# A decoder block in fp32: the row sums of four modulation vectors, as fp32 products in the array's column groups

## The chip, the cores and the metric

The kernel runs on one core of a Trainium2 chip (trn2). A core has five engines that run side by side and wait for one another by semaphores: TensorE (PE; its weight load is listed as PEld), VectorE (DVE), ScalarE (ACT), GpSimd (POOL) and SyncE (SP), which here only issues DMAs. The metric is device time in microseconds, from start to end of one execution.

## What is computed

A decoder block on 512 tokens of width 1024. A conditioning vector c gives six modulation vectors, each of 1024 elements, with a full matrix product per vector. Two of them (shift and scale of the first norm) are needed at once; the other four (g1, sh2, sc2, g2) only from the output projection on.

```python
c_act = jax.nn.silu(c)
mod = (c_act @ w_mod[l] + b_mod[l])[:, None, :]
sh1, sc1, g1, sh2, sc2, g2 = jnp.split(mod, N_MOD, axis=-1)
h = rms_norm(x) * (1.0 + sc1) + sh1
proj = h @ w_in[l]
u, v, z, xbc, dt_raw, gate_a, gate_b = jnp.split(proj, offs, axis=-1)
...
mixed = (jax.nn.sigmoid(gate_a) * (y_a @ w_branch_gm[l])
         + jax.nn.sigmoid(gate_b) * (y_b @ w_branch_ssm[l]))
x = x + g1 * (mixed @ w_out[l])
h2 = rms_norm(x) * (1.0 + sc2) + sh2
x = x + g2 * (jnp.square(jax.nn.relu(h2 @ w_ff1[l])) @ w_ff2[l])
```

## The kernel before

All large products run in three parts: a weight is split into a high part (wH, a cast by ScalarE) and a low part (wL, the difference, by VectorE, or by GpSimd for the weights in POOL_L), the activations likewise, and `mm3` adds high x high, high x low and low x high in PSUM. Weights come in pieces of 1 MB, two pieces ahead of their use (AHEAD = 2, line 26); `weight` (line 164) and `emit_w` (line 142) issue load, cast and difference. The pieces lie in a ring of three raw buffers (`rawt`), and the split halves in rings of four.

`projA` (line 180) makes one block of 128 output columns: 8 blocks of K, three products each, so 24 products of 512 columns. A piece of 256 columns gives two such blocks, called b = 0 and b = 1.

The stretch of the change is a loop over eight pieces: ("ga", 0), ("ga", 1), ("gm", 0), ("ga", 2), ("gm", 1), ("ga", 3), ("gm", 2), ("gm", 3). The "ga" pieces are the gate of the gMLP branch, the "gm" pieces its branch product. The SSM part follows, with pieces bc0, xs0, z0 and so on. Into this loop the remaining modulation vectors are woven: after block b = 0 of each piece `mod2(q)` (line 623) is called, with q = 0 to 7; each q is one half (512 elements) of one vector.

Small works are placed by hand: `later(n, fn)` (line 121) puts fn on a list, due n units from now; `tick` (line 124) advances the time by half a unit, in the middle and at the end of each projA, and runs what is due. So one unit is one projA, and one piece is two units. TensorE's instructions keep exactly the order in which the program issues them (class InOrder). VectorE, ScalarE and SP had that order forced for the first stage only; from then on a scheduler orders each engine's queue at compile time, by the order of issue and by what it takes to be ready. On the chip every queue is strictly in order.

`mod2(q)` before: two loads of 1 MB (w_mod rows 0 to 511 and 512 to 1023, 512 columns), in two of the three raw buffers; eight VectorE steps, each raw row block times a column of the activated c, added alternately to two accumulators; GpSimd adds the two (line 638). The partition sum is still to be taken. `finish`, three units later, splits the accumulator in m2H (ScalarE) and m2L (VectorE). `rows`, three units after that, multiplies both with a matrix of ones (two products of 512 columns), and VectorE adds the bias row br, and 1 for the sc2 vector. The row goes to DRAM, to `grow`, from where it is read back, spread over the partitions, before the output projection (line `g1row = rowload(grow[0], "g1")` and the next ones). br is loaded from b_mod in `mod2`.

Others that matter here. `dt_phase` (line 693) computes softplus and the running sum of dt by about twenty small VectorE steps, each dependent on the one before; it is issued right after `mod2(0)`. Its `to_tok` transposes the results (copies cumt and dtt), its `lasts` uses cumt. `mod_rows` (line 312) makes the first two modulation vectors at the start of the kernel by fp32 products in column groups: 32 columns of weights each, at `tile_position=(0, 32 * j)`. `decays` (line 779) has GpSimd subtract and mask the tile cum. PSUM has five banks for `mm` and three for `sx` (row sums, transposes, SSM).

Of the kernel before, what the change touches and what calls it, by code (L numbers as in the profile page):

```python
# [11 lines left out]
ALU = mybir.AluOpType  # L12
# [3 lines left out]
P = 128  # L16
S = 512
D = 1024
# [14 lines left out]
def hybrid_block(ctx: ExitStack, tc: tile.TileContext, x, c, w_mod, b_mod, w_in, gm_norm_w, gm_ws,  # L33
# [3 lines left out]
    pool = nc.gpsimd  # L37
# [20 lines left out]
    pe, dve, act = InOrder(nc.tensor, True), InOrder(nc.vector, True), InOrder(nc.scalar, True)  # L58
    sp = InOrder(nc.sync, True)
# [8 lines left out]
    def nm(s):  # L68
        uid[0] += 1
        return f"{s}_{uid[0]}"  # L70

    def const(shape, name, dt=F32):
        return cst.tile(shape, dt, tag=name, name=name)

    def blk(name, dt=F32, n=512):
        return big.tile([P, n], dt, tag="b", name=nm(name), bufs=NB)
# [7 lines left out]
    def rawt(name):  # L84
        return big.tile([P, 2048], F32, tag="raw", name=nm(name), bufs=3)
# [6 lines left out]
    def mm_bank():  # L92
        return psp.tile([P, 512], F32, tag="mm", name=nm("mm"), bufs=5)

    def sx_bank():
        return psp.tile([P, 512], F32, tag="sx", name=nm("sx"), bufs=3)
# [7 lines left out]
    def stt(o, a, s, b, op0, op1):  # L104
        dve.scalar_tensor_tensor(o, in0=a, scalar=s, in1=b, op0=op0, op1=op1)

    def low(L, src, H, eng=None):
        (eng or dve).tensor_tensor(L, in0=src, in1=H.bitcast(F32), op=ALU.subtract)  # L108

    def split(src, name):  # L110
        H, L = blk(name + "H", F32R), blk(name + "L", F32R)
        act.copy(H, src)
        low(L, src, H)
        return H, L

    mm, tr = pe.matmul, pe.transpose
# [4 lines left out]
    def later(n, fn):  # L121
        pend.append((unit[0] + n, fn))
# [88 lines left out]
    for f in range(2):  # L211
        for j in range(8):
            c0 = f * 2048 + j * 256
# [39 lines left out]
    ones = const([P, P], "ones")  # L253
# [3 lines left out]
    onesr = const([P, P], "onesr", F32R)  # L257
# [39 lines left out]
    cact = const([P, KB], "cact")  # L297
# [49 lines left out]
    def mod_sum(k):  # L347
        ps = sx_bank()
        for a in range(2):
            mm(ps[:, a:a + 1], lhsT=accm[k][:, a * P:(a + 1) * P], rhs=ones[:, 0:1], start=True, stop=True)  # L350
        return ps
# [147 lines left out]
    for k in range(1, KB - 1):  # L499
# [18 lines left out]
        else:  # L518
            mains(k, 2, B7)
            ps = mod_sum(k + 1)  # L520
# [53 lines left out]
    for h in range(2):  # L574
        w = weight(("v1", h)) if h else wv[0]
        for k in range(4):
            wh, wl = w(k, 0, 512)
            kk = 4 * h + k
# [38 lines left out]

    grow = drm.tile([4, D], F32, name="grow")

    def small_row(name):  # L620
        return blk(name)[0:1, :]

    def mod2(q):
        which, half = divmod(q, 2)
        c0 = (2 + which) * D + half * 512
        acc = [blk("acc"), blk("acc")]
        for j2 in range(2):
            raw = rawt("mod2").rearrange("p (k n) -> p k n", k=4)
            sp.dma_start(raw, w_mod[0][j2 * 512:(j2 + 1) * 512, c0:c0 + 512].rearrange("(k p) n -> p k n", p=P))
            for j in range(4):  # L630
                kk = j2 * 4 + j
                a = acc[j % 2]
                if kk < 2:
                    dve.tensor_scalar(a, in0=raw[:, j], scalar1=cact[:, kk:kk + 1], scalar2=None, op0=ALU.mult)
                else:
                    stt(a, raw[:, j], cact[:, kk:kk + 1], a, ALU.mult, ALU.add)

        pool.tensor_tensor(acc[0], in0=acc[0], in1=acc[1], op=ALU.add)
        br = small_row("br")
        sp.dma_start(br, b_mod[0:1, c0:c0 + 512])  # L640

        def finish():
            H, L = split(acc[0], "m2")
            later(3, lambda: rows(H, L))

        def rows(H, L):
            ps = sx_bank()
            mm(ps, lhsT=onesr, rhs=H, start=True, stop=False)
            mm(ps, lhsT=onesr, rhs=L, start=False, stop=True)
            stt(br, ps[0:1, :], 1.0 if which == 2 else 0.0, br, ALU.add, ALU.add)  # L650
            sp.dma_start(grow[which:which + 1, half * 512:(half + 1) * 512], br)
        later(3, finish)


    yaH, yaL = [None] * 8, [None] * 8
# [19 lines left out]
    for j in range(3):  # L675
        w = weight(("u", j))
        for b in range(2):
            ps = mm_bank()
# [69 lines left out]
    for kind, j in (("ga", 0), ("ga", 1), ("gm", 0), ("ga", 2), ("gm", 1), ("ga", 3), ("gm", 2), ("gm", 3)):  # L748
        w = weight((kind, j))
        for b in range(2):  # L750
            m = 2 * j + b
            ps = mm_bank()
            if kind == "ga":
                projA(ps, w, b * P, hH, hL)
                ga[m] = blk("ga")
                act.activation(ga[m], ps, AF.Sigmoid)
            else:
                projA(ps, w, b * P, yaH, yaL)
                pa[m] = ga[m]
                mul(ga[m], ps, ga[m])  # L760
            if b == 0:
                mod2(nmod[0])
                nmod[0] += 1
            tick()
# [167 lines left out]
    for j in range(4):  # L932
        w = weight(("gb", j))
        for b in range(2):
            ps = mm_bank()
# [14 lines left out]
    for j in range(4):  # L950
# [5 lines left out]
        for b in range(2):  # L956
# [3 lines left out]
            H, L = split(gb[m], "mx")  # L960
# [62 lines left out]
    for t in range(NT):  # L1023
        ps = mm_bank()
# [44 lines left out]
    for f in range(2):  # L1069
# [13 lines left out]
        for j in range(j0, 8):  # L1083
            w = weight(("f1", f, j))
            for b in range(2):
                ps = mm_bank()
# [4 lines left out]
        for n in range(2):  # L1091
# [4 lines left out]
            for qp in range(2):  # L1096
# [7 lines left out]
                for k, (t, i, c0, c1) in steps:  # L1104
                    wh, wl = ws[k // 4](k % 4, c0, c1)
                    kk = 8 * qp + k
# [38 lines left out]
```

## Time and profile before

| what | value |
|---|---|
| median of 3 runs | 1098.85 us (1096.06 to 1101.81) |
| profiled execution | 1096.96 us |
| its span, first to last instruction | 1095.3 us |
| mean granted TensorE clock | 0.997 of full speed |
| busy: PE, DVE, ACT, POOL | 98%, 60%, 44%, 17% of the span |

The profile is one execution. "Busy" counts the time in which an engine has an instruction in it; products overlap in the array, so that 512 columns are listed with 390 ns and yet follow one another every 0.23 us. "PE sx L49" means an instruction of TensorE that writes a bank named sx; most lines are 49, the line of the helper that records all operations, so groups are told apart by their tiles. In the chain (the work that ended last, followed back) each piece is released by the one before it. "x48" means that 48 instructions are drawn together in one row; the time is then from the first one's start to the last one's end. In brackets stands the idle time before, and what ended it.

### The profile page before, as it was taken

How to read it: one execution, taken by the hardware profiler on the slowest of the kernel's cores; microseconds unless marked ns; L12 is line 12 of the kernel's file. 1: busy time of each engine (PE TensorE's matmuls, PEld its weight loads, DVE VectorE, ACT ScalarE, POOL GpSimd, SP SyncE). 2: the span in 40 equal slices, each digit the busy share in tenths (PEclk: the TensorE clock that was granted, in tenths of full speed). 3: DMA queues.
4: the chain of work that ended last, by engine and by line, in shares of the span. 5: the costliest groups of instructions: out<-in, count | busy, mean ns of one | idle time of the engine just before them, and what ended most of it. 6: DMA issues, size and time to landing. Idle time of an engine off the chain costs nothing.

```text
span 1095.3 us, 13316 instructions
## 1 busy us (share of the span) xinstructions
PE 1075.7 (98%) x5330; PEld 895.6 (82%) x5330; DVE 652.2 (60%) x897; ACT 482.5 (44%) x637; POOL 186.5 (17%) x131
## 2 busy tenths in 40 slices
PE   8999999999999999999999999989999999999997
PEld 7788887888888888888888888878888888888886
DVE  4854699976687677687757434385443425444244
ACT  5557345355665655655537222233432112433122
POOL 0030743132431431431110000350000000000000
PEclk9999999999999999999999999999999999999999
DMA  9863257985343333333333234313232323232302
GB/s 296 261 196 97 75 180 271 316 257 166 116 126 107 116 125 106 116 125 106 106 115 115 77 116 135 115 43 116 93 112 81 113 80 116 77 115 96 115 1 78
DMA packets 122623, 141.67 MB, mean 129 GB/s; under 512 B 3664, under 2 KB 93856, under 8 KB 122560
## 3 DMA queue, kind: packets, MB, share of 16 engines
q1 hardware_dynamic: 120768, 137.09, 39.9%
q10 hardware_dynamic: 1152, 2.10, 0.5%
q0 software_dynamic: 640, 1.63, 0.5%
q8 instruction: 42, 0.69, 0.3%
q14 instruction: 21, 0.17, 0.0%
HBM read 138.55 MB, written 2.24 MB: 129 GB/s over the span
## 4 chain that ended last, share of the span: by engine, by line
PE 90%; DVE 6%; DMA 2%; ACT 1%; issue 1%; POOL 0%; DVEq 0%; ACTq 0%; POOLq 0%
PE mm L49 75%; PE sx L49 15%; DMA mod<-in_w_mod_dram 1%; DVE xn L49 1%; DVE acc L49 1%; DVE e L49 1%; DMA brow<-in_b_mod_dram 0%; DVE xr L49 0%; POOL wL L108 0%; DVE q L49 0%; ACT junk L49 0%; DVE ss L49 0%; DVE h L49 0%; DVE s L49 0%; ACT h L49 0%
## 5 line engine op out<-in xcount | busy, mean ns | idle before, releaser
L49 PE MATMUL mm<-h,wH 128*128 128x512 f32 (+1 forms) x1712 | 521.6, 386 | 0.0
L49 PEld LDWEIGHTS mm<-h,wH 128*128 128x128 f32 x1712 | 312.8, 189 | 61.0 <-issue 2.7
L49 PE MATMUL mm<-h,wL 128*128 128x512 f32 (+1 forms) x856 | 327.9, 383 | 1.4 <-POOL wL L108 1.4
L49 DVE TENSOR_TENSOR wL<-raw,wH 128x1024 fp32r<-128x1024 f32 x154 | 194.0, 1263 | 207.0 <-ACT wH L49 206.8
L49 ACT CAST wH<-raw 128x1024 fp32r<-128x1024 f32 x170 | 177.5, 1049 | 294.2 <-PE mm L49 223.6
L49 PEld LDWEIGHTS mm<-h,wL 128*128 128x128 f32 x856 | 161.3, 188 | 34.0 <-POOL wL L108 1.6
L49 ACT ACT_TABLE_LOAD x64 | 82.1, 1283 | 6.2 <-issue 3.0
L49 DVE SCALAR_TENSOR_TENSOR cv<-mm,wcol,cv 128x511 f32<-128x511 f32 (+2 forms) x96 | 70.9, 743 | 13.7 <-ACT cv L49 13.1
L49 PE MATMUL mm<-wL,aH 128*128 128x512 f32 (+1 forms) x176 | 66.8, 380 | 0.0
L49 PE MATMUL mm<-wH,aH 128*128 128x512 f32 (+1 forms) x176 | 66.8, 380 | 0.0
L49 PE MATMUL mm<-wH,aL 128*128 128x512 f32 (+1 forms) x176 | 66.8, 379 | 0.0
L108 POOL TENSOR_TENSOR wL<-raw,wH 128x1024 fp32r<-128x1024 f32 x16 | 40.7, 2548 | 130.7 <-ACT wH L49 130.5
L794 POOL TENSOR_TENSOR cum<-cum,cumt 128x1024 f32<-128x1024 f32 x16 | 34.7, 2166 | 71.5 <-DMA cum<-cumd 58.3
L49 DVE TENSOR_TENSOR r<-r 128x512 f32<-128x512 f32 x32 | 22.0, 688 | 35.7 <-ACT r L49 35.7
L49 PE MATMUL mm<-wH,h 128*128 128x512 f32 x128 | 40.2, 401 | 0.9 <-ACT h L49 0.9
L49 PE MATMUL mm<-y,wH 128*128 128x512 f32 x128 | 39.4, 389 | 0.0
L49 PEld LDWEIGHTS mm<-wH,aL 128*128 128x128 f32 x176 | 33.1, 188 | 6.3
L49 PEld LDWEIGHTS mm<-wH,aH 128*128 128x128 f32 x176 | 33.1, 188 | 5.9
L49 PEld LDWEIGHTS mm<-wL,aH 128*128 128x128 f32 x176 | 33.1, 188 | 5.9
L49 ACT ACTIVATE r<-mm 128x512 f32<-128x512 f32 x32 | 19.0, 594 | 39.5 <-PE mm L49 39.5
L49 DVE SCALAR_TENSOR_TENSOR acc<-mod,cact,acc 128x512 f32<-128x512 f32 x48 | 35.5, 791 | 0.5 <-DMA mod<-in_w_mod_dram 0.5
L49 PE MATMUL sx<-wL,aH 128*128 128x512 f32 (+1 forms) x96 | 35.7, 372 | 0.0
(236 smaller groups left out, 1519.2 us busy)
## 6 DMA issues: line engine op xcount, KB each, us to landing
raw<-in_w_ff_dram SPq DMA_DIRECT2D x32, 1024.0 KB, 5.1
raw<-in_w_in_dram SPq DMA_DIRECT2D x28, 1024.0 KB, 5.5
mod<-in_w_mod_dram SPq DMA_DIRECT2D x16, 1024.0 KB, 7.0
raw<-in_w_in_dram SPq DMA_DIRECT2D x18, 512.0 KB, 4.1
mod<-in_w_mod_dram SPq DMA_DIRECT2D x16, 512.0 KB, 7.3
cum<-cumd SPq DMA_DIRECT2D x16, 512.0 KB
raw<-in_w_branch_ssm_dram SPq DMA_DIRECT2D x8, 1024.0 KB, 5.2
raw<-in_w_branch_gm_dram SPq DMA_DIRECT2D x4, 1024.0 KB, 6.1
```

The source lines that it names most:

```text
L49: r = fn(*a, **k)
L108: (eng or dve).tensor_tensor(L, in0=src, in1=H.bitcast(F32), op=ALU.subtract)
L794: pool.tensor_tensor(cv, in0=cv, in1=ct, op=ALU.subtract)
```

## The change

Each q now has one accumulator: the first step writes it, the other seven add to it, one after another. GpSimd's sum, the split in m2H and m2L and the function `finish` are gone. After q = 3 and after q = 7, three units later, `rows` takes four accumulators at once: four fp32 products, each with a 128 x 32 matrix of ones, in the four column groups, all into one bank; so vector j of the four stands in partitions 32j to 32j + 31. One VectorE step over 128 partitions adds the four bias rows and `plus1`, a small constant that holds 1 for the sc2 rows. The four bias rows are now loaded within `rows`, each spread over 32 partitions, and four rows go to `grow`.

```diff
-    def small_row(name):
-        return blk(name)[0:1, :]
+    plus1 = const([P, 2], "plus1")
+    pool.memset(plus1, 0.0)
+    pool.memset(plus1[0:64, 1:2], 1.0)
...
-        acc = [blk("acc"), blk("acc")]
+        acc = blk("acc")
...
-                a = acc[j % 2]
-                if kk < 2:
-                    dve.tensor_scalar(a, in0=raw[:, j], scalar1=cact[:, kk:kk + 1], scalar2=None, op0=ALU.mult)
+                if kk == 0:
+                    dve.tensor_scalar(acc, in0=raw[:, j], scalar1=cact[:, kk:kk + 1], scalar2=None, op0=ALU.mult)
                 else:
-                    stt(a, raw[:, j], cact[:, kk:kk + 1], a, ALU.mult, ALU.add)
-
-        pool.tensor_tensor(acc[0], in0=acc[0], in1=acc[1], op=ALU.add)
-        br = small_row("br")
-        sp.dma_start(br, b_mod[0:1, c0:c0 + 512])
-
-        def finish():
-            H, L = split(acc[0], "m2")
-            later(3, lambda: rows(H, L))
-
-        def rows(H, L):
-            ps = sx_bank()
-            mm(ps, lhsT=onesr, rhs=H, start=True, stop=False)
-            mm(ps, lhsT=onesr, rhs=L, start=False, stop=True)
-            stt(br, ps[0:1, :], 1.0 if which == 2 else 0.0, br, ALU.add, ALU.add)
-            sp.dma_start(grow[which:which + 1, half * 512:(half + 1) * 512], br)
-        later(3, finish)
+                    stt(acc, raw[:, j], cact[:, kk:kk + 1], acc, ALU.mult, ALU.add)
+        m2acc.append(acc)
+        if q % 4 == 3:
+            later(3, lambda: rows(q // 4, m2acc[q - 3:]))
+
+    m2acc = []
+
+    def rows(b, accs):
+
+        br = blk("br")
+        ps = sx_bank()
+        for j in range(4):
+            c0 = 2 * D + (4 * b + j) * 512
+            sp.dma_start(br[32 * j:32 * (j + 1)], b_mod[0, c0:c0 + 512].partition_broadcast(32))
+            mm(ps[32 * j:32 * (j + 1), :], lhsT=ones[:, 0:32], rhs=accs[j], start=True, stop=True,
+               tile_position=(0, 32 * j))
+        stt(br, ps, plus1[:, b:b + 1], br, ALU.add, ALU.add)
+        for j in range(4):
+            which, half = divmod(4 * b + j, 2)
+            sp.dma_start(grow[which:which + 1, half * 512:(half + 1) * 512], br[32 * j:32 * j + 1])
```

## Rows read from the trace of the kernel before

**Rows 1.** The page's chain that ended last: share of the span by engine.
```profile
PE 90%; DVE 6%; DMA 2%; ACT 1%; issue 1%; POOL 0%; DVEq 0%; ACTq 0%; POOLq 0%
```

**Rows 2.** Waits of TensorE, whole span: for whom, us in total, times, longest.
```profile
PE sx L49 <- DVE xn L49: 4.1, 1, 4.1
PE mm L49 <- POOL wL L108: 1.4, 1, 1.4
PE sx L49 <- DVE dtt L49: 1.3, 1, 1.3
...
PE sx L49 <- DVE m2L L49: 0.9, 1, 0.9
```

**Rows 3.** Pieces of the chain between 120 and 260 us: start, us, what.
```profile
133.94 5.08 DMA mod<-in_w_mod_dram
...
165.07 7.54 DMA mod<-in_w_mod_dram
...
182.06 10.93 PE mm L49 x48
```

**Rows 4.** TensorE in order of time: start us, us, what it writes and reads.
```profile
167.03 0.40 PE L49 MATMUL sx<-m2H,onesr 128*128 128x512 f32 x1
...
168.69 0.63 PE L49 MATMUL mm<-h,wH 128*128 128x512 f32 x2
...
179.67 0.39 PE L49 MATMUL mm<-yaH,wL 128*128 128x512 f32 x1
...
181.90 0.40 PE L49 MATMUL mm<-yaH,wH 128*128 128x512 f32 x1
...
212.84 0.39 PE L49 MATMUL mm<-yaH,wH 128*128 128x512 f32 x1
```

**Rows 5.** TensorE at the start of the kernel: the products of mod_rows(0), what follows.
```profile
13.45 1.07 PE L49 MATMUL sx<-mod,cact 128*32 128x256 f32 x16
14.45 1.16 PE L49 MATMUL sx<-ones 128*128 128x128 f32 x8
```

**Rows 6.** VectorE in order of time: dt phase, accumulations, a pair of wL, cv.
```profile
145.81 2.94 DVE L49 TENSOR_TENSOR s<-e,q 32x512 f32<-32x512 f32 x1
...
149.95 8.43 DVE L49 SCALAR_TENSOR_TENSOR e<-e,q 32x512 f32<-32x512 f32 x6
...
175.72 5.29 DVE L49 SCALAR_TENSOR_TENSOR acc<-mod,cact,acc 128x512 f32<-128x512 f32 x4
...
188.04 2.72 DVE L49 SCALAR_TENSOR_TENSOR acc<-mod,cact,acc 128x512 f32<-128x512 f32 x4
...
201.32 3.18 DVE L49 TENSOR_TENSOR wL<-raw,wH 128x1024 fp32r<-128x1024 f32 x2 [0.41 <-ACT wH L49]
...
229.13 0.67 DVE L49 SCALAR_TENSOR_TENSOR br<-sx,br 1x512 f32<-1x512 f32 x1
229.73 2.72 DVE L49 SCALAR_TENSOR_TENSOR acc<-mod,cact,acc 128x512 f32<-128x512 f32 x4
232.38 1.52 DVE L49 SCALAR_TENSOR_TENSOR cv<-mm,wcol,cv 128x511 f32<-128x511 f32 x2
```

**Rows 7.** GpSimd in order of time.
```profile
141.93 1.56 POOL L638 TENSOR_TENSOR acc<-acc,acc 128x512 f32<-128x512 f32 x1 [4.89 <-DVE nega L49]
...
151.00 5.41 POOL L108 TENSOR_TENSOR wL<-raw,wH 128x1024 fp32r<-128x1024 f32 x2 [2.80 <-ACT wH L49]
...
175.72 1.92 POOL L794 TENSOR_TENSOR cum<-cum,cumt 128x1024 f32<-128x1024 f32 x1 [4.01 <-DVE cumt L49]
```

**Rows 8.** SP's queue: the second load of vector 3.
```profile
182.16 0.37 SPq L49 DMA_DIRECT2D mod<-in_w_mod_dram  x1
```

**Rows 9.** The small load brow of b_mod: from issue to landing.
```profile
DMA to landing us min/median/max: 4.8/4.8/4.8
```

**Rows 10.** Stretches: busy us (instructions) of PE, PEld, DVE, ACT, POOL; PEclk; DMA.
```profile
740.00:746.00 6.00, 5.13 (x31) 4.92 (x32) 3.33 (x6) 1.17 (x2) 0.00 (x0) 0.72 0.65 226
730.00:735.00 5.00, 4.32 (x33) 3.93 (x34) 4.93 (x4) 0.00 (x0) 5.00 (x4) 1.00 0.67 206
```

## Prediction

> **What bounds the kernel now.** I read the chain that ended last first, its shares and then its pieces, next TensorE's waits, then the stretch that the change touches, engine by engine. The chain lies 90% on TensorE [rows 1]. So an edit is worth the TensorE time it takes away or adds, instructions and waits, and nothing done by VectorE, ScalarE, GpSimd or the queues counts before TensorE waits for it. Before the MLP TensorE hardly waits, yet two of its few waits lie at the old row sums: 0.92 us for m2L of vector 0, 1.30 us for a bank that the copy dtt had to free [rows 2]. The chain there leaves TensorE: it runs through the dt phase on VectorE, a mod load of 7.54 us, vector 2's accumulation, and comes back to TensorE at 181.35; from there on it is TensorE alone, 10.9 us per 48 products, through all later row sums [rows 3]. Hence up to 181 us this stretch is tied to VectorE and the mod loads, after that to TensorE. In what follows q0 to q7 are the eight half vectors, acc(q) their accumulators, and "load a" and "load b" the first and second 1 MB load of each.
>
> **What goes from TensorE.** The pair of q0 costs 1.66 us from its first product to the next projection product (167.03 to 168.69) with the wait in it. That of q1 costs 2.00 us, from 179.90 (one pitch of 0.23 after the product at 179.67) to 181.90 [rows 4]. The other six pairs wait for nothing: TensorE's waits name no third one, and two products at the pitch of the stream, 0.228 us (48 in 10.93 [rows 3]), are 0.46 us, so 2.8 us for six. Together 6.4 us.
>
> **What is added on TensorE.** Two sets of four fp32 products of 512 columns in four column groups. The nearest row is the early row products: eight fp32 products of 256 columns, recorded as 16, over the same four groups; the next work starts 1.00 us after the first of them [rows 5]. Two rounds of 256 columns are one of 512, so a set costs 1.0 us, 2.0 for both. The change of tiling on the way in and out is in that row. If all waits vanished, the sum would be 2.0 - 6.4 = -4.4 us.
>
> **Where the first set lands.** This decides. The order of TensorE is fixed as written. q3's accumulation is issued after the first half of weight ("ga", 2); three units later is the middle of the second half of ("gm", 1). Before, q3's sum came six units after. From 181.90 it is 24 products of the stream further, so that place is at 187.35 in the trace of before; with 3.66 us gone ahead of it TensorE is there at about 183.7. It then needs acc(3) whole. In the trace of before the last four steps of acc(3) run from 188.04 to 190.76 [rows 6]. So a set placed three units after waits, unless VectorE and the loads come several us earlier.
>
> **When acc(3) is ready after the change.** One accumulator makes each step depend on the one before. Two dependent steps (cv at 232.38) take 1.52 us together, four alternating ones, from 229.73 to 232.38, 2.65 [rows 6]; that is a pitch of 0.76 to 0.78, with which I go on, against 0.66. A half vector is then 0.5 + 7 x 0.78 = 6.0 us instead of 4.8, with its first half 2.85 and its second 3.1. That adds 9.5 us to VectorE over the eight; taking away eight m2L and eight br steps at about 0.60 (229.13 to 229.73) gives 9.6 back, and two new br steps cost 1.5. VectorE is not relieved as a whole. Upstream sits the dt phase. The GpSimd sum of acc(0) at 141.93 stands ahead of a pair of wL [rows 7], which hold up VectorE's s<-e,q to 148.75, and a second pair at 151.00 holds up two of the six e steps, which take 8.43 us together [rows 6]. Without that sum the first pair can go about 1.9 us earlier; the second pair is set by its casts and stays, and catches the fifth and sixth e step instead of the third and fourth, so that 1.4 us are left. q1 then starts at 161.4 instead of 162.86. Now the loads: two raw buffers alternate, so load a of q2 is issued when q1's first half is consumed (164.3). By its row it takes 7.5 us [rows 3], less a little: 171.5. q2's first half ends at 174.35, cumt costs 0.25, the second half takes 3.1 us plus the 2.57 that the same four steps lost beside GpSimd's cum (5.29 instead of 2.72) [rows 6, 7]: 180.3. Only then is load b of q3 issued. A load of this size landed after 5.08 us at 133.94, and the one issued at 182.16 was there for the step at 188.04, so within 5.9 [rows 3, 6, 8]; I take 5.9: 186.2. VectorE is free by then (a pair of wL, at most 3.2 as at 201.32, and q3's first half, 2.85). Four steps more: **acc(3) at 189.3.** Bounds: 186 (nothing lost beside GpSimd, landing in 5.1, VectorE the limit) and 192.9 (no gain in the dt phase, both loads at 7.5).
>
> The Trainium skill, "SBUF — State Buffer", section "Who interferes with whom", has VectorE operations with two SBUF inputs and GpSimd operations exclude each other for whole instructions. By it the removed GpSimd sum is a gain for the dt phase; without it acc(3) would come 1.4 us later, and the sum below would be 4.4 instead of 3.0. The rows at 145.81 and 149.95 agree: each stretch ends only when the pair beside it does [rows 6, 7].
>
> **The sum.** The first three products of the set run at 183.7 and are over by 184.7. The fourth runs alone, two records, the length of the whole set: TensorE goes on at 189.3 + 0.1 + 1.0 = 190.4, which is 3.05 us after the 187.35 of before. It idles 4.6 us. After its longest wait, 4.1 us for xn up to 740.4 [rows 2], the granted clock fell to the lower of its two levels, 1.2 GHz. From 740 to 746 the mean was 0.72, so 1.7 us were lost [rows 10]. TensorE's next longest wait, 1.4 us before 730.45, had no such fall behind it (1.00 from 730 to 735); nothing lies between [rows 2, 10]. I count 1.7. Then the six pairs give back 2.8 and the second set costs 1.0: +3.05 + 1.7 - 2.8 + 1.0 = **+3.0 us.** The profiled execution took 1096.96 us (span 1095.30 and 1.66 around it), 1.89 below the median of 1098.85; so 1100 by that execution, and 1101.8 on the median, which I predict.
>
> **What is taken at nothing.** ScalarE loses eight casts; it idles for TensorE and for loads here, as the chain without it shows. SP stood in its queue before eight grow stores that wait for br; they now stand in two clumps, and mod loads no longer queue behind them (the one at 182.16 could have gone at 181.0; inside the bounds). The eight br loads move from mod2 into rows: at SP they may come behind q4's loads, at about 190.7. The small brow load took 4.8 us [rows 9], the slowest mod load 7.5, so br lands at 195.5 to 198.2 and VectorE may sit at the new br step for 5 to 8 us, with q4's steps and wL behind it. The cover is wL of gm3: written from 201.32 on, 3.2 us long, read by TensorE from 212.84 [rows 4, 6], 8 us of slack, to which the later TensorE adds its own 3. Beyond that each us is a us. The sx bank stays held meanwhile; until the SSM part asks for banks the other two are free. The second set comes in the middle of the second half of bc0, near 234; acc(7) was complete at 232.45 [rows 6] and has 1.2 us more of chain, so its wait is 0 to 1.5 us; I take 0. GpSimd's two memsets come ahead of its wL, each a fraction of a us.
>
> **Rivals.** First, no wait: VectorE, freed of m2L and br early, has acc(3) by 183.7. Then the sum is -4.4: 1094.4. For it speaks VectorE's unbroken busy time up to 200; against it that the path to acc(3) holds two loads of which none gets shorter. If acc(3) comes at 186 instead, the result is -2.0 (1096.8). Chance of this side 0.17. Second, slower: the load path holds at its slow end, load b of q3 issued after 182 and 7.5 us long, q1 not earlier. acc(3) at 192.9 makes TensorE go on at 194.0: +6.65 + 1.7 - 1.8 = +6.55, 1105.4; with the wait of the second set 1107. It decides from acc(3) at 191.85 on. For it speaks the load at 165.07, against it the two quick ones. Chance 0.18. Third, the change does not pack: four fp32 products one after another would cost about 4 us per set instead of 1, +6 in all. The 16 records in 1.00 us [rows 5] speak against it: 0.03. The forecast, a wait of 2 to 7 us that eats the gain, has 0.62.
>
> **How the numbers follow.** Half a per cent, 5.5 us, is about what a measurement of this kernel can tell from no change. Even the best case, -4.4, does not reach it except with some help from noise: faster 0.06. Slower is the second and third rival and the upper end of the forecast: 0.20. Within: 0.74. For 8 in 10 I go from near the no-wait case to past the slow one: 1095 to 1106.5.
>
> **What would show it.** After the change TensorE's waits must name acc with 2 to 7 us at the first set, at about 184, and a clock below 1 right behind it. m2L and dtt must be gone from the waits. Each set must span about 1 us. mod's second load of q3 must be issued when q2's last step ends. I am wrong if TensorE passes the first set without waiting, if VectorE takes acc(2) and acc(3) in another order, or if SP's br loads hold VectorE so long that a wL is late.

## The result and the profile after

The changed kernel took 1108.99 us (median of 4 runs, 1108.69 to 1109.45) against 1098.5 us of the kernel before. The ratio is 1.0099, with a 95% interval from 1.0082 to 1.0115: 10.5 us slower by the medians, where 3 us were forecast, and beyond the range. The profiled execution has a span of 1107.1 us, 11.8 more than before. "Vector 3" below is the half vector q3 of the prediction, and so for the others.

The chain that ended last and the waits of TensorE after (whom it waited for: us in total, times, longest):

```profile
PE 88%; DVE 9%; ACT 1%; issue 1%; DMA 1%; ACTq 0%; DVEq 0%
```
```profile
PE sx L49 <- DVE acc L49: 10.0, 2, 8.6
...
PE sx L49 <- DVE cum L49: 1.2, 1, 1.2
```

VectorE's share of the chain rose from 6% [rows 1] to 9%. The waits for m2L and dtt [rows 2] are gone; in their place stand two waits for acc, 8.6 and 1.4 us, and a new one of 1.2 us for cum, at the transposes of the dt phase. TensorE in order of time:

```profile
184.94 1.56 PE L49 MATMUL sx<-acc,ones 128*32 128x512 f32 x6
195.06 1.92 PE L49 MATMUL sx<-acc,ones 128*32 128x512 f32 x2 [8.56 <-DVE acc L49]
196.90 0.80 PE L49 MATMUL mm<-yaH,wH 128*128 128x512 f32 x1
...
201.62 0.63 PE L49 MATMUL mm<-h,wH 128*128 128x512 f32 x2
...
242.55 1.06 PE L49 MATMUL sx<-acc,ones 128*32 128x512 f32 x6
245.01 1.05 PE L49 MATMUL sx<-acc,ones 128*32 128x512 f32 x2 [1.40 <-DVE acc L49]
```

Three products of the first set run at 184.94 (each is recorded as two); the fourth starts at 195.06, when the last step of acc(3) has ended. It takes 1.92 us alone, where the fourth of the second set takes 1.05. The twelve products after it take 4.72 us (196.90 to 201.62) instead of 2.73. The stretches of 1 us show why (columns as in [rows 10]):

```profile
190.00:191.00 1.00, 0.00 (x0) 0.00 (x0) 1.00 (x2) 0.00 (x0) 0.00 (x0) 0.84 0.97 279
191.00:192.00 1.00, 0.00 (x0) 0.00 (x0) 0.93 (x3) 0.00 (x0) 0.00 (x0) 0.50 1.06 377
...
200.00:201.00 1.00, 1.00 (x4) 0.75 (x3) 0.00 (x0) 0.00 (x0) 0.00 (x0) 0.54 0.25 68
201.00:202.00 1.00, 1.00 (x6) 0.82 (x5) 0.18 (x1) 0.35 (x1) 0.00 (x0) 1.00 0.00 0
```

TensorE had nothing from 186.5 on; the granted clock fell to its lower level, 1.2 GHz, between 190 and 191, still within the wait, and came back to 2.4 GHz between 200 and 201.

Against the kernel before, TensorE stands like this. At the place of the first set it is 2.4 us early (184.94 against 187.35). Behind the set it is 9.55 late, and at the first product of ga3 11.5 late (201.62 against 190.10). Four quiet pairs of sums that are no longer there bring it to 9.7 at the second set (242.55 against 232.87, the place 24 products behind vector 5's pair). That set costs 3.4 us in all (the next product starts at 245.99), which makes 13.1; two more pairs and small things leave 11.8 at the end.

VectorE, GpSimd and SP in the stretch that leads to acc(3):

```profile
140.79 3.66 DVE L49 SCALAR_TENSOR_TENSOR acc<-mod,cact,acc 128x512 f32<-128x512 f32 x2
144.37 2.60 DVE L49 TENSOR_SCALAR q<-e 32x512 f32<-32x512 f32 x1
...
151.17 2.78 DVE L49 TENSOR_TENSOR q<-s 32x512 f32<-32x512 f32 x1
153.98 2.51 DVE L49 TENSOR_SCALAR e<-q 32x512 f32<-32x512 f32 x1
...
165.25 0.47 DVE L49 TENSOR_SCALAR acc<-mod,cact 128x512 f32<-128x512 f32 x1
...
174.77 0.49 DVE L49 TENSOR_SCALAR acc<-mod,cact 128x512 f32<-128x512 f32 x1 [1.04 <-DMA mod<-in_w_mod_dram]
...
176.23 8.30 DVE L49 SCALAR_TENSOR_TENSOR acc<-mod,cact,acc 128x512 f32<-128x512 f32 x5
...
188.54 0.48 DVE L49 TENSOR_SCALAR acc<-mod,cact 128x512 f32<-128x512 f32 x1
...
190.33 4.68 DVE L49 SCALAR_TENSOR_TENSOR acc<-mod,cact,acc 128x512 f32<-128x512 f32 x6
```
```profile
141.50 5.20 POOL L108 TENSOR_TENSOR wL<-raw,wH 128x1024 fp32r<-128x1024 f32 x2 [4.45 <-ACT wH L49]
...
175.53 2.36 POOL L797 TENSOR_TENSOR cum<-cum,cumt 128x1024 f32<-128x1024 f32 x1 [19.32 <-DVE cumt L49]
...
179.36 2.35 POOL L797 TENSOR_TENSOR cum<-cum,cumt 128x1024 f32<-128x1024 f32 x1
```
```profile
168.11 0.39 SPq L49 DMA_DIRECT2D mod<-in_w_mod_dram  x1
...
169.74 1.19 SPq L49 DMA_DIRECT2D cum<-cumd  x1
...
179.96 5.83 SPq L49 DMA_DIRECT2D mod<-in_w_mod_dram  x2
```

Without GpSimd's sum the pair of wL goes at 141.50, and the pair holds up the last step of acc(0) and q<-e; the next pair holds up q<-s and e<-q. Vector 1 starts at 165.25 (before: 162.86). Load a of vector 2 is issued at 168.11 and lands for the step at 174.77. The five steps of vector 2 from 176.23 on take 8.30 us, where six steps beside no GpSimd work take 4.68: GpSimd now does two cum tiles there, before it was one [rows 7]; the load of the second one is issued at 169.74, before it was at 223.12. The first step of acc(0), the first of vector 1 and that load in the kernel before:

```profile
134.38 2.94 DVE L49 TENSOR_SCALAR acc<-mod,cact 128x512 f32<-128x512 f32 x2
...
162.86 0.86 DVE L49 TENSOR_SCALAR acc<-mod,cact 128x512 f32<-128x512 f32 x2
```
```profile
223.12 0.78 SPq L49 DMA_DIRECT2D cum<-cumd  x1
```

Vector 3 starts at 188.54, and acc(3) is complete at 195.0. VectorE then waits 5.66 us, up to 201.82, for a product of TensorE that stands behind the set (ga<-mm,ga), so vector 4 and the later ones are late by TensorE's wait as well.

### The profile page after: what moved, and what is told of

It reads as the page before. It is cut to its first block, busy times and chain, and to the rows that moved or that the text cites. A ratio compares the mean times of both kernels' runs of the same rounds, so it can differ in the third digit from the quotient of the medians.

```text
span 1107.1 us, 13268 instructions
## 1 busy us (share of the span) xinstructions
PE 1079.1 (97%) x5330; PEld 894.5 (81%) x5330; DVE 653.3 (59%) x883; ACT 472.2 (43%) x624; POOL 174.9 (16%) x125
## 4 chain that ended last, share of the span: by engine, by line
PE 88%; DVE 9%; ACT 1%; issue 1%; DMA 1%; ACTq 0%; DVEq 0%
PE mm L49 74%; PE sx L49 15%; DVE acc L49 3%; DVE xn L49 1%; DVE q L49 1%; DVE e L49 1%; DMA mod<-in_w_mod_dram 1%; DVE xr L49 0%; ACT junk L49 0%; DVE wL L49 0%; DVE ya L49 0%; DVE ss L49 0%; DVE h L49 0%; ACT h L49 0%; DVE r L49 0%
## 5 line engine op out<-in xcount | busy, mean ns | idle before, releaser
L49 PEld LDWEIGHTS mm<-h,wL 128*128 128x128 f32 x856 | 161.4, 189 | 33.9 <-POOL wL L108 1.7
L49 DVE SCALAR_TENSOR_TENSOR acc<-mod,cact,acc 128x512 f32<-128x512 f32 x56 | 49.4, 882 | 1.5
```

The source lines that it names most:

```text
L49: r = fn(*a, **k)
```

## The experiments

Theory W: the loss is TensorE's wait for acc(3), with a lesser one for acc(7), at places too close behind the last accumulation, and the lower clock that follows. Theory C: the chain of eight dependent steps slows VectorE's stream and costs wherever the sets stand. Theory G: GpSimd's early cum tiles make acc(3) late. Ratios are to the kernel before.

### Both sets six units after the last accumulation

```diff
-            later(3, lambda: rows(q // 4, m2acc[q - 3:]))
+            later(6, lambda: rows(q // 4, m2acc[q - 3:]))
```

> The changed kernel with both sets of four products six units after the last accumulation instead of three, the distance that the old sums had. Theory W (the loss is TensorE's wait for acc(3), and a lesser one for acc(7), with the lower clock behind it): both waits go, the sets cost 1.0 us each, the six quiet pairs and the two old waits are saved; with the 1.2 us that TensorE newly waits for the dt phase this is 3 us less than before, a ratio of 0.997, and 14 us less than the changed kernel. Theory C (the dependent chain of eight steps slows VectorE's whole stream): TensorE still waits for acc or for wL by several us, ratio 1.003 or more.

Measured: 0.9956 (0.9941 to 0.9971), 1093.68 us, span 1092.4. TensorE in order of time, and VectorE's steps of vector 3:

```profile
165.25 0.24 PE L49 MATMUL sx<-ident,cum 32*128 32x32 f32 x1 [1.16 <-DVE cum L49]
...
201.75 1.06 PE L49 MATMUL sx<-acc,ones 128*32 128x512 f32 x8
...
246.86 1.06 PE L49 MATMUL sx<-acc,ones 128*32 128x512 f32 x8
```
```profile
191.15 4.68 DVE L49 SCALAR_TENSOR_TENSOR acc<-mod,cact,acc 128x512 f32<-128x512 f32 x6
```

VectorE is as late as in the changed kernel (acc(3) at 195.8), and yet TensorE waits for no acc: eight records of a set in 1.06 us, both times. All of the loss, and a gain besides, hangs on the place. This kernel is faster than both the one before and the changed one.

### Vector 3 alone three units after, in the kernel before

```diff
-            later(3, lambda: rows(H, L))
+            later(1.5 if q == 3 else 3, lambda: rows(H, L))
...
-        later(3, finish)
+        later(1.5 if q == 3 else 3, finish)
```

> The kernel before with one edit: vector 3 (q = 3) alone is split and summed by the old pair of products three units after its accumulation instead of six. Nothing is packed, no chain of eight, GpSimd's sum stays. Theory W (the distance of three units is too short at this place, whatever is summed): in the trace of before acc(3) is complete at 190.8, with GpSimd's sum, the cast and m2L at about 193.4, and TensorE comes at 187.3; so it waits 6 us there and then pays for the lower clock as the changed kernel did, 2 us: ratio 1.006 to 1.008. If it is the chain or the packing that costs: 1.000.

Measured: 1.0064 (1.0041 to 1.0087). TensorE, and a stretch with the clock (last but two columns):

```profile
193.30 0.79 PE L49 MATMUL sx<-m2H,onesr 128*128 128x512 f32 x1 [5.28 <-ACT m2H L49]
```
```profile
190.00:196.00 6.00, 2.70 (x6) 1.88 (x7) 4.32 (x7) 1.56 (x2) 1.26 (x1) 0.51 0.99 348
```

A wait of 5.28 us at that place, the lower clock behind it, and 7 us lost, with the old pairs of products, two accumulators and GpSimd's sum. So neither packing nor chain is needed for the loss.

### The second set alone at three units

```diff
-            later(3, lambda: rows(q // 4, m2acc[q - 3:]))
+            later(6 if q == 3 else 3, lambda: rows(q // 4, m2acc[q - 3:]))
```

> The changed kernel with the first set at six units and the second left at three. With both at six, acc(7) was complete at 238.1, and the place three units earlier is reached by TensorE at 230.5. Theory W: the second set alone makes TensorE wait about 7 us, after which the clock is low: 7.5 + 2 to 3 us above the kernel with both at six, ratio 1.004 to 1.005; the second set was as badly placed as the first, and the changed kernel hid that because the first wait had given VectorE time. If the second set's wait is a mere 1.4 us as in the changed kernel: 0.997.

Measured: 1.0060 (1.0044 to 1.0077). TensorE, and a stretch:

```profile
201.95 1.06 PE L49 MATMUL sx<-acc,ones 128*32 128x512 f32 x8
...
230.38 1.06 PE L49 MATMUL sx<-acc,ones 128*32 128x512 f32 x6
237.90 1.91 PE L49 MATMUL sx<-acc,ones 128*32 128x512 f32 x2 [6.47 <-DVE acc L49]
```
```profile
234.00:240.00 6.00, 2.10 (x3) 0.43 (x4) 5.01 (x8) 2.96 (x3) 0.00 (x0) 0.58 1.12 326
```

The second place is bad too: 6.47 us of waiting by itself, where the first had 8.56, and a span 10.0 us above that of the kernel with both sets at six (1102.4 against 1092.4). In the changed kernel it cost 1.4 us of waiting only: TensorE came there 12.2 us later (242.55 instead of 230.38), and acc(7) only 7.2 us later (245.0 instead of 237.8). The first set alone at three units was not run.

### Two accumulators, summed in the array, at three units and at six

```diff
-        acc = blk("acc")
+        acc = [blk("acc"), blk("acc")]
...
-            mm(ps[32 * j:32 * (j + 1), :], lhsT=ones[:, 0:32], rhs=accs[j], start=True, stop=True,
-               tile_position=(0, 32 * j))
+        for i in range(2):
+            for j in range(4):
+                mm(ps[32 * j:32 * (j + 1), :], lhsT=ones[:, 0:32], rhs=accs[j][i], start=i == 0, stop=i == 1,
+                   tile_position=(0, 32 * j))
```

> The changed kernel with two alternating accumulators as before, summed in the array: eight products per set instead of four, place unchanged at three units. Theory W: each half vector takes 4.8 instead of 6.0 us and the dt phase starts 2 us earlier, so acc(3) is ready about 4 us earlier, at 191; TensorE still waits there 4 us, a set costs 2 us instead of 1: ratio about 1.005. Theory C: the time falls back to that of before or below, ratio 1.000 or less.

Measured at three units: 0.9983 (0.9973 to 0.9992), so Theory C's number and not W's. TensorE and VectorE:

```profile
187.01 1.90 PE L49 MATMUL sx<-acc,ones 128*32 128x512 f32 x10 [1.52 <-DVE acc L49]
```
```profile
135.14 2.95 DVE L49 TENSOR_SCALAR acc<-mod,cact 128x512 f32<-128x512 f32 x2
...
163.55 0.86 DVE L49 TENSOR_SCALAR acc<-mod,cact 128x512 f32<-128x512 f32 x2
...
183.56 4.06 DVE L49 SCALAR_TENSOR_TENSOR acc<-mod,cact,acc 128x512 f32<-128x512 f32 x6
```

acc(3) came at 187.6, not at the 191 expected: 7.4 us earlier than in the changed kernel. The chain itself is about 1.2 us per vector; the rest is what comes with it upstream, a dt phase that ends later and a second cum tile beside vector 2, which is not there in this kernel. Most of it lies in vector 2: its first step is 1.5 us earlier than in the changed kernel (173.32 against 174.77), its last one ends 6.1 earlier (179.3 against 185.4). The compiler ordered the queues of this kernel anew, so the lengthening by the chain and the other order are not told apart. Here C was right, as far as the sets stand at three units.

> Both sets at six units and two alternating accumulators, summed in the array by eight products per set. Theory W: no wait for acc with either accumulation, so the chain costs nothing once the sets are late; eight products cost 1 us more per set, and the 1.2 us that TensorE waits for the dt phase are gone: 0.8 us above the kernel with both at six and one accumulator, ratio 0.996 to 0.997. Theory C (the chain costs by itself): 2 us or more below it, ratio 0.994 or less.

Measured at six units: 0.9966 (0.9952 to 0.9980), against 0.9956 with one accumulator. The two intervals overlap. TensorE waits for no acc either way, and the second four products of a set cost their own time, 1.92 us per set instead of 1.06, as W had it. What the chain costs with late sets is the wait of 1.16 us for cum at the transposes, which the trace with two accumulators does not have; beyond that these runs show it to matter only through the time at which acc(3) is complete.

### The loads of decays(0) behind the last mod load

```diff
-    decays(0)
+    with tc.issue_after(m2load[0]):
+        decays(0)
```

(m2load[0] is the last mod load that SP issued.)

> The changed kernel with the loads of decays(0) queued behind the last mod load, so that GpSimd's two subtractions and masks on cum, which ran at 175 to 183 us beside the accumulation of vector 2, run after the loop. Theory G (that GpSimd work is what makes acc(3) so much later than predicted): the five steps that took 8.3 us take 3.9, ScalarE's casts for ga3 come earlier, acc(3) is ready 4 to 5 us earlier, ratio 1.004 to 1.006. If the lateness comes from the dt phase and the loads alone: acc(3) moves by less than 1 us, ratio 1.009 or more.

Measured: 1.0085 (1.0064 to 1.0105). VectorE and TensorE:

```profile
178.10 3.11 DVE L49 SCALAR_TENSOR_TENSOR acc<-mod,cact,acc 128x512 f32<-128x512 f32 x4 [1.85 <-DMA mod<-in_w_mod_dram]
```
```profile
190.81 1.92 PE L49 MATMUL sx<-acc,ones 128*32 128x512 f32 x2 [5.21 <-DVE acc L49]
...
243.22 1.05 PE L49 MATMUL sx<-acc,ones 128*32 128x512 f32 x2 [4.00 <-DVE acc L49]
```

Without the cum tiles the steps go at 0.78 each, and acc(3) comes at 190.8, 4.3 us earlier: Theory G is right on that. But the time hardly moved. The second set now waits 4.00 us instead of 1.40, and the last steps of vector 7 run beside the cum tiles, which had been moved to just there. TensorE leaves the first set 4.3 us earlier than in the changed kernel (192.65 against 196.90) and the second only 1.8 earlier (244.20 against 245.99); behind it the granted clock falls too (0.50 from 245 to 246), and 48 products further on 0.2 us are left (256.85 against 257.02). What one wait gives, the next takes.

### Filling the wait

```diff
+            if b == 0 and j == 3:
+                spin(32, sx_bank())
             mm(ps[32 * j:32 * (j + 1), :], lhsT=ones[:, 0:32], rhs=accs[j], start=True, stop=True,
```

> The changed kernel with 32 small idle products of ones (0.25 us each, 8 us) between the third and the fourth product of the first set; nothing is left out. They run while TensorE would wait for acc(3). Theory W with its clock part: the wait stays in length but TensorE is not idle, the granted clock stays at 1.00, and the 2.9 us that the lower clock cost behind the wait (0.9 in the last product, 2.0 in the twelve after it) come back: ratio 1.007. If the clock costs nothing: the same as the changed kernel, 1.010.

Measured: 1.0109 (1.0090 to 1.0128), within error the changed kernel's. TensorE, and a stretch:

```profile
186.83 7.41 PE L49 MATMUL sx<-ones 128*128 128x128 f32 x64
195.46 1.05 PE L49 MATMUL sx<-acc,ones 128*32 128x512 f32 x2 [1.22 <-DVE acc L49]
196.44 0.50 PE L49 MATMUL mm<-yaH,wH 128*128 128x512 f32 x1
...
199.30 0.62 PE L49 MATMUL mm<-h,wH 128*128 128x512 f32 x2
...
243.61 1.52 PE L49 MATMUL sx<-acc,ones 128*32 128x512 f32 x2 [2.35 <-DVE acc L49]
```
```profile
190.00:196.00 6.00, 4.78 (x40) 4.18 (x39) 5.82 (x9) 1.04 (x1) 0.00 (x0) 1.00 0.99 313
```

With work in the wait the clock stays at 1.00; the last product takes 1.05 us instead of 1.92, the twelve after it 2.86 instead of 4.72. That is the 2.7 us the clock cost at the first set, 2.3 of them left at ga3 (199.30 against 201.62). Again they are not in the total: the second set is reached 2.35 us earlier and left only 0.9 earlier, and the next stretch gives up the rest (48 products in 12.20 us instead of 11.12), with the clock at 0.50 from 245 to 247. In the changed kernel it was 1.00 from 242 to 250. The clock's price is shown; that it lengthens the changed kernel is not.

### One GpSimd addition put back

```diff
+        if q == 0:
+            pool.tensor_tensor(blk("twice"), in0=acc, in1=acc, op=ALU.add)
         m2acc.append(acc)
```

> The changed kernel plus one GpSimd addition after vector 0 (acc(0) + acc(0) into a tile that nobody reads), at the place where the removed GpSimd sum of acc(0) stood; nothing is left out. It must wait for acc(0) and so holds GpSimd's pair of wL back, which in the changed kernel began at 141.5 and stopped the last step of acc(0) and the first of the dt phase. Theory L (the removed sum had kept GpSimd off VectorE's way; without it the dt phase ends later): the last step of acc(0) takes 0.8 instead of 2.9 us, vector 1 starts at about 163 instead of 165.2, and acc(3) comes 2 us or more earlier than 195.0. Theory of the prediction (the removed sum is a gain of 1.4 us for the dt phase): vector 1 starts at 166 or later.

Measured: 1.0061 (1.0044 to 1.0078). VectorE, GpSimd and TensorE:

```profile
136.40 8.41 DVE L49 SCALAR_TENSOR_TENSOR acc<-mod,cact,acc 128x512 f32<-128x512 f32 x7
```
```profile
140.60 2.88 POOL L108 TENSOR_TENSOR wL<-raw,wH 128x1024 fp32r<-128x1024 f32 x1 [3.08 <-ACT wH L49]
144.96 1.04 POOL L638 TENSOR_TENSOR twice<-acc 128x512 f32<-128x512 f32 x1 [1.48 <-DVE acc L49]
```
```profile
193.06 1.92 PE L49 MATMUL sx<-acc,ones 128*32 128x512 f32 x2 [7.60 <-DVE acc L49]
```

The addition did not take the old place: one half of the pair of wL went ahead of it and still held up acc(0). The order of VectorE's queue changed too, so this run does not show what the addition does by itself. It is inconclusive on Theory L: vector 1 starts at 164.69, between the two values expected. In this kernel useless GpSimd work went with an acc(3) 2 us earlier and a time some 4 us shorter than the changed kernel's, so an addition near that place is at least no sure loss.

### The transposes of the dt phase one unit later

```diff
-        later(5, to_tok)
+        later(6, to_tok)
```

(with both sets at six units)

> Both sets at six units, one accumulator, and the transposes of the dt phase one unit later (six instead of five). The only wait of TensorE that the late sets left in this stretch is 1.2 us for cum at those transposes. It should go: 1.2 us less than the kernel with both at six, ratio 0.9945. If the dt phase delays VectorE for others, no change: 0.9956.

Measured: 0.9981 (0.9968 to 0.9993), against 0.9956 (0.9941 to 0.9971) without the edit: no gain, and probably a loss, though the two intervals overlap a little.

```profile
177.27 0.49 PE L49 MATMUL sx<-cumt,sel 128*128 128x128 f32 x2 [2.21 <-DVE cumt L49]
```

The 1.16 us at the transposes went, and 2.21 us came at `lasts`, which needs the copy cumt and stayed where it was. I had not counted that follower.

## Why the prediction was wrong

**The step that failed** is the one that the prediction calls deciding: when acc(3) is ready. It was put at 189.3 and was 195.0; the wait of the second set, put at 0, failed with it. In the terms of the sum: the first set cost +9.55 us instead of +3.05 (0.9 of it in the lone product at the lower clock), the slower products behind it 2.0 where the clock was put at 1.7, the second set 3.4 instead of 1.0, and the six pairs gave back the 2.8. That makes 12.2, and the span 11.8.

**The mechanism was right.** The named place, three units after the last accumulation, is where the time went; a wait for acc with the clock below 1 behind it, though of 8.56 us where 2 to 7 were named; m2L and dtt gone from the waits; a set of four in 1.06 us; load b of vector 3 issued when vector 2's last step ended (185.4). The sum without a wait, -4.4 us, was close too: with the 1.2 us for cum it gives -3.2, and both sets at six units gave 2.9 us in the span and 4.8 by the ratio.

**The terms that were mis-sized**, largest first:

- "acc(3) at 189.3": it was 195.0, +5.7 us, beyond the upper bound of 192.9. The first piece of it is "1.4 us are left. q1 then starts at 161.4". It started at 165.25. The gain from the removed GpSimd sum never came. In the kernel with two accumulators and no GpSimd sum, vector 1 starts 28.4 us after the first step of acc(0) (135.14 to 163.55); before it was 28.5 (134.38 to 162.86). The pair of wL did go earlier, as said, but it now met acc(0)'s last step and q<-e, and the second pair met q<-s and e<-q, not the fifth and sixth e step. In the changed kernel four VectorE operations stood for about 2.1 us each behind GpSimd; before, three did, and with two accumulators it is three again, so the fourth comes with the chain. The sum of the prediction also left the chain out of acc(0), which stands ahead of the dt phase: with the held step it ended at 144.4, before at 141.8. And only the two held e steps end about when the pair beside them does (157.0 and 156.4), not the whole stretch of six, which ends at 158.4. The rule of the Trainium skill ("SBUF — State Buffer", "Who interferes with whom") agrees with these rows (a held operation takes 2.5 to 2.9 us, the same ones unheld 0.4 to 0.8); what failed is the sum that I drew from it, which moved GpSimd's pair and left VectorE's operations where they were.
- "the 2.57 that the same four steps lost beside GpSimd's cum": five steps lost 4.4 us, because the second cum tile ran there too. The compiler's order had put its load at 169.74 instead of 223.12. The run with decays(0) held back shows the size: acc(3) 4.3 us earlier.
- "its wait is 0 to 1.5 us; I take 0" for the second set: 1.4 us, and the fourth product alone behind it, 3.4 us for the set instead of 1.0. I took acc(7) at its time in the kernel before and counted 1.2 us for the chain. In the changed kernel it came at 245.0 instead of 232.45: VectorE was late already at acc(3), and then waited 5.66 us for TensorE. The second set alone at three units, where TensorE does not wait at the first, still waits 6.5 us: vector 7 starts at 230.26 there, before at 226.41, and three cv steps of the next piece go between its steps.
- "I count 1.7" for the clock: 2.7 at the first set (0.9 in the lone product and 1.9 behind it, against the run with the wait filled). The row that I took, behind a wait of 4.1 us, has no such lone product in it. The length of the wait did not set the price in these runs: behind the 5.21 us of the run with decays(0) held back the same products took 1.92 and 4.61 us, behind 8.56 us 1.92 and 4.72.

**The second rival**, the slow end of the load path, was the right side but not the right cause: its loads were not slow (6.6 us for load a of vector 2); VectorE was. Its price of +6.55 would have been reached from acc(3) at 192.9.

**What was taken at nothing** held for br: VectorE did its br step at 208.6 without waiting for it. The wait for cum at the transposes, 1.2 us, was not in the list at all, nor was the other order in which the compiler put the loads of decays(0).

**What stays open.** Whether the removed GpSimd sum acted as a guard of VectorE before, or whether the compiler's other order of VectorE's queue did it: the run that put an addition back does not separate them. Nor is it known how much of the lateness of acc(3) the chain causes by its length and how much the other order of the queues that came with it, or which distance between three and six units would do.

## What to carry to other kernels

When an in-order engine gets a step that needs several results at once, it waits for the latest; here the distance that each sum had had alone, six units, was enough, and half of it was not. The gap can be read before the change, between the last row of the producer and the place in the consumer's queue. A dependent chain cost little here while its reader came late (1.2 us, at another reader behind it), and more than its own length once the reader came early; and time gained before a second such wait was given back there, so count on to the next place where the engine waits; and where the producer itself waits for that engine, as VectorE does here, it comes late there too.

## What the runs showed of the hardware

- Four fp32 products of 512 columns with 32 columns of weights each, in four column groups, took 1.06 us together; a single one took 1.05 us. The groups cost 0.01 us on top of one product.
- Dependent VectorE steps on one fp32 accumulator of 128 x 512 followed each other at 0.78 us (six in 4.68), alternating ones on two accumulators at 0.66 (six in 4.06).
- A VectorE operation with a single tensor input stood behind GpSimd as long as those with two: q<-e took 2.60 us beside a pair of wL, and 0.41 in the kernel with one GpSimd addition put back, where it started just ahead of a wL. The Trainium skill ("SBUF — State Buffer", "Who interferes with whom") names tensor_scalar among the operations that can take the shared ports, and the row agrees.
